# Adding a bias by accumulating DMAs at the end of a decoder trunk, and sharing one normalisation between two engines

## The chip, the cores and the metric

The kernel runs on one core of a Trainium2 chip. The core has five engines with instruction streams of their own: TensorE (PE; its weight loads are listed apart as PEld), VectorE (DVE), ScalarE (ACT), GpSimd (POOL) and SyncE (SP, which here only issues DMAs). Sixteen DMA engines move data between HBM and the on-chip memory (SBUF). Matmuls write their results to a third memory, PSUM. The metric is the device time of one execution in microseconds; the kernel before takes 1242.96 us (median of three runs, 1242.6 to 1243.46).

## The reference

A two-layer trunk for 256 tokens of width 2048. Layer 0 is a Mamba-2 mixer, layer 1 a dilated windowed attention; between them the residual stream gives one shared K and V. Each layer ends in the same layer norm. Cut to what the change touches:

```
def _layer_norm(x, g, b):
    mu = jnp.mean(xf, -1, keepdims=True)
    var = jnp.mean(jnp.square(xf - mu), -1, keepdims=True)
    return ((xf - mu) * lax.rsqrt(var + LN_EPS)) * g + b
...
for layer in range(DEPTH):
    shift, scale, gate = _adaln(c, ada_w[layer], ada_b[layer])
    h = x * (1.0 + scale) + shift
    y = _ssd_mixer(h, ...) if layer == 0 else _dilated_mixer(h, k_sh, v_sh, ...)
    x = _layer_norm(ALPHA * x + (1.0 + gate) * y, ln_g[layer], ln_b[layer])
    if layer == 0:
        k_sh, v_sh = _shared_kv(x, kv_w)
```

The output is the second layer norm: for each token the normalised row, times `ln_g[1]`, plus `ln_b[1]`.

## The kernel before

All matrix products are made from float32 operands split into a rounded high part and a remainder. `split` (L95 to L102) does this for each weight piece of 128x1024: ACT writes `whi` (L99), DVE writes `wlo` (L101). The helpers `tm_mults` (L212 to L214) and `cm_wide` (L181, L184) multiply the pieces. Weight pieces come in one after the other on SP's DMA queue.

The 256 tokens are handled as two blocks b = 0 and b = 1 of 128 rows; block b holds the tokens 2j + b, so that a block's rows are every second row of the output. `u[0]` and `u[1]` hold the residual stream of the two blocks, 128x2048 each; in the instruction listings they are `u_5515` and `u_5516`. A chunk is 512 of the 2048 columns.

The order of the instructions on each engine is fixed when the program is built. It follows the code, except that a scheduler may move an instruction ahead of others that it doesn't depend on; `tc.issue_after(x)` tells it to keep what is built inside behind the instruction x. At run time each engine works through its list in order and waits on semaphores.

Two places matter here.

The first is the end of layer 0. `residual` (L798 to L800) makes gate times product plus residual for each chunk and collects its statistics; `moments` (L802 to L813) turns these into a factor and an offset per row. `normalise(b, c0_, c1_)` (L819 to L824) applies them to some columns: on ACT (L822) or on DVE (L824). The first 512 columns of a block are normalised in two calls of 256 columns, the other 1536 columns later in three calls. Then `x_quad(b)` has TensorE transpose the first four 128-column tiles (L885), ACT write their scaled high part (L887), ACT or DVE write the full value (L890, L892), and DVE the remainder (L893). With that, the products for V begin: `high` (L915) and `low` (L920) multiply the four tiles by weight pieces split in advance, first for block 0, then for block 1. After that a loop over q = 2 to 7 goes on with `split` and `tm_mults`, and `x_tile` makes the further tiles, two for each q (L871, L874 to L876).

The second is the end of the kernel. The last products of block 0 end earlier than those of block 1. `r0, nb0` are block 0's factor and offset: ACT normalises its four chunks (L1138), and for each chunk DVE multiplies by `ln_g[1]` (`scaled`, L1105), DVE adds `ln_b[1]` (L1158), and SP stores the chunk (L1130). At the same time block 1 is finished: its last products, its residual (L798, L799), its statistics (L800), and `moments`. Three of block 1's chunks take another way: TensorE adds up the scaled residual and minus the mean (L1151, L1155) in PSUM, and one DVE instruction applies the factor and adds `ln_b[1]` (`whole`, L1163). The fourth is normalised by ACT (L1160), multiplied by DVE (L1105) and added to by DVE (L1170). `lnt[:, 0]` and `lnt[:, 1]` hold `ln_g[1]` and `ln_b[1]`, repeated on all 128 partitions (L1119); in the listings they are part of `actT`.

Of the kernel before, what the change touches and what calls it, by code (L numbers as in the profile page):

```python
# [13 lines left out]
ALU = mybir.AluOpType  # L14
# [35 lines left out]
def trunk(ctx, tc, xT, x, c, par, cst, bias, lnrow, ada, wdt, win, wxs, wout, wk, wv, wbin, wbout, out):  # L50
    nc = tc.nc
    V, S, T, PO = nc.vector, nc.scalar, nc.tensor, nc.gpsimd
# [9 lines left out]
    def bcast(dst, src, off=0):  # L62
        nc.sync.dma_start(dst, bass.AP(tensor=src.tensor, offset=src.offset + off,
                                       ap=[[0, P], [1, dst.shape[-1]]]))
# [22 lines left out]
    def rows(t, b):  # L87

        return t.rearrange("(j r) n -> r j n", r=2)[b]

    def load_piece(src):
        raw = wp.tile([P, 1024], F32, name="raw", bufs=6)
        nc.sync.dma_start(raw, src)
        return raw

    def split(raw, into=None, after=None):

        hi, lo = into or [wp.tile([P, 1024], F32R, name=n, bufs=4) for n in ("whi", "wlo")]
        copied.append(S.activation(hi, raw, AF.Copy))  # L99
        with tc.issue_after(after) if after is not None else ExitStack():  # L100
            latest.append(V.tensor_tensor(lo, raw, hi.bitcast(F32), op=ALU.subtract))  # L101
        return hi.rearrange("p (k n) -> p k n", k=2), lo.rearrange("p (k n) -> p k n", k=2)  # L102
# [114 lines left out]
    def tm_pair():  # L217
        return [mm.tile([P, 512], F32, name="acc") for _ in range(2)]
# [92 lines left out]
    def queue(pool, cols):  # L311

        loaded = [ada_load(pool, *cols[0])]

        def step(i):
            raw = loaded.pop(0)
            if i + 1 < len(cols):
                loaded.append(ada_load(pool, *cols[i + 1]))
            ada_dot(*cols[i], raw)

        jobs.extend(lambda i=i: step(i) for i in range(len(cols)))

    def drain():
        while jobs:
            jobs.pop(0)()
# [8 lines left out]
    with ExitStack() as cA:  # L334
# [458 lines left out]
        u = [pu.tile([P, D], F32, name=f"u{b}") for b in range(2)]  # L793
# [24 lines left out]

        def normalise(b, c0_, c1_):  # L819
            (r, nb), cs_ = norm[b], slice(c0_, c1_)  # L820
            if b == 0 or c1_ <= 512:
                S.activation(u[b][:, cs_], u[b][:, cs_], AF.Identity, bias=nb, scale=r)  # L822
            else:
                V.tensor_scalar(u[b][:, cs_], u[b][:, cs_], r, nb, op0=ALU.mult, op1=ALU.add)  # L824
# [76 lines left out]
    def evict_v(hq, g, ps):  # L901
        vt[hq, g] = place(3 * hq + g if hq == 0 else 9 + g, [P, 2, 512])
        with behind_next():
            for b in range(2):
                S.activation(vt[hq, g][:, b, :], ps[b], AF.Copy)

    with ExitStack() as cL:
        pl = cL.enter_context(tc.tile_pool(name="pl", bufs=3))

        vps = [tm_pair(), tm_pair()]  # L910
        def high(i, b):
            for k in range(2):
                kt = 2 * (i // 2) + k
                for w in first_v[i]:
                    T.matmul(vps[i % 2][b], hx(kt)[:, b * P:b * P + P], w[:, k, :], start=kt == 0 and w is first_v[i][0],  # L915
                             stop=False)

        def low(i, b):
            for k in range(2):
                T.matmul(vps[i % 2][b], lx(2 * (i // 2) + k)[:, b * P:b * P + P], first_v[i][0][:, k, :], start=False,  # L920
                         stop=False)

        end, _ = x_quad(0)
        with tc.issue_after(end.ins):
            for n in range(1, 4):
                normalise(0, 512 * n, 512 * n + 512)
        for i in range(4):
            high(i, 0)
        for i in range(4):
            if i == 2:  # L930
                _, tile4 = x_quad(1)
                for n in range(1, 4):
                    normalise(1, 512 * n, 512 * n + 512)
            low(i, 0)
        for i in range(4):
            high(i, 1)
            if i == 2:
                x_tile(4)
                x_tile(5)
        for i in range(4):  # L940
            low(i, 1)
        for q in range(2, KT // 2):
            if q < KT // 2 - 1:
                x_tile(2 * q + 2)
                x_tile(2 * q + 3)
            for j in range(2):
                w = split(load_piece(wv[2 * j][q]), after=tile4.ins if q == 2 else None)
                tm_mults(q, w, vps[j], hx, lx, 0, KT, range(2))
        for g in range(2):
            evict_v(0, g, vps[g])  # L950

        R = (1, 2)
        pin[0] = latest[-1].ins
        with tc.issue_after(tile4.ins):
            state[0] = 0
            queue(pl, cols1[11:])
            jobs.append(lambda: gate_out(1))
            upcoming.extend((wk[2 * (2 * g + hq) + w], 0) for hq in range(2) for g in range(NG) for w in range(2))
            upcoming.extend((wv[1 + 2 * g], 0) for g in range(NG))
            evict_v(0, 2, tm_chunk(wv[4], hx, lx, rate=R))  # L960
            for hq in range(2):
                for g in range(NG):
                    kv[hq, g] = place(3 + 3 * hq + g, [P, 4, L])
                    for w in range(2):
                        cm_wide(wk[2 * (2 * g + hq) + w], kv[hq, g][:, 2 * w:2 * w + 2, :], rate=R, later=True)
            for g in range(NG):
                evict_v(1, g, tm_chunk(wv[1 + 2 * g], hx, lx, rate=R))
            drain()
            late = latest[-1].ins

        ada_bias(1, slice(0, KT), slice(0, 2))
        for kt in range(KT):
            t = pl.tile([P, L], F32, name="htmp")
            S.activation(t, xhi[:, kt, :].bitcast(F32), AF.Identity, bias=shift(1, kt), scale=scale(1, kt))
            V.scalar_tensor_tensor(t, xlo[:, kt, :].bitcast(F32), scale(1, kt), t, op0=ALU.mult, op1=ALU.add)
            split_act(xhi[:, kt, :], xlo[:, kt, :], t)
# [119 lines left out]
    gt, lnt = gl[:, 0], gl[:, 1]  # L1096
# [19 lines left out]
    for i in range(2):  # L1116
        hold(6 + i)
        with tc.issue_after(latest[-1].ins):
            bcast(lnt[:, i, :], lnrow, (2 + i) * D)  # L1119
    for n in range(2):  # L1120
        scaled(1, chunk[n])
    ps = [tm_pair() for _ in range(2)]
# [6 lines left out]
    def store(b, c):  # L1129
        nc.sync.dma_start(rows(out, b)[:, c], u[b][:, c])  # L1130
# [12 lines left out]
    for h in range(2):  # L1143
        end = last(1, 1, slice(256 * h, 256 * h + 256), halves[h])
# [10 lines left out]
        T.matmul(pt, diag, lnt[:, 0, c], start=False, stop=True)  # L1155
    for c in chunk:
        scaled(0, c)
        V.tensor_tensor(u[0][:, c], u[0][:, c], lnt[:, 1, c], op=ALU.add)  # L1158
        store(0, c)
    S.activation(u[1][:, chunk[3]], u[1][:, chunk[3]], AF.Identity, bias=nb1, scale=r1)  # L1160

    def whole(n):
# [100 lines left out]
```

## Time and profile before

| | |
|---|---|
| median of 3 runs | 1242.96 us (1242.6 to 1243.46) |
| the profiled execution | 1243.02 us, of which its span takes 1241.2 us |
| TensorE busy | 1216.1 us, 98% of the span |
| VectorE busy | 1028.3 us, 83% |
| ScalarE busy | 702.4 us, 57% |
| GpSimd busy | 0.2 us, 4 instructions |
| granted TensorE clock | 1.0 over the whole execution |

A row of the timeline reads: start in us from the span's start, duration in us, engine, line of the kernel, operation, what is written from what, number of instructions merged into the row, and in brackets how long the engine stood idle before it and what ended the wait. On one engine successive instructions overlap a little, so that they start closer together than their durations say. A row with SPq is the issue of a DMA, not its transfer; the time "to landing" is given apart. In the row of a window the columns are its length, the busy time and number of instructions of PE, PEld, DVE, ACT and POOL, then the granted clock, the mean busy share of the DMA engines, and the GB/s that they moved.

### The profile page before, as it was taken

To read this page: it belongs to the slowest core of one execution; us is meant where nothing else is said; L and a number is where in the kernel's file an instruction comes from. 1 tells how busy PE (TensorE), PEld (TensorE's weight loads), DVE (VectorE), ACT (ScalarE), POOL (GpSimd) and SP (SyncE) were. 2 spreads that over 40 slices of the span, in tenths; PEclk is the share of its full clock that TensorE was granted. 3 is DMA by queue.
4 is the path that set the end of the run, shared out by engine and by line. 5 is a ranking of instruction groups with operands and counts; after the bars stand their busy time and mean duration, and the time that the engine had idled before them with its cause. 6 is when DMAs were issued, how large, how long until landed. Compare 5 with 4: busy or idle time off the path is not lost.

```text
span 1241.2 us, 18711 instructions
## 1 busy us (share of the span) xinstructions
PE 1216.1 (98%) x7078; PEld 1043.9 (84%) x7078; DVE 1028.3 (83%) x1454; ACT 702.4 (57%) x1045; POOL 0.2 (0%) x4
## 2 busy tenths in 40 slices
PE   4999999999999999999999999999999999999997
PEld 4989988898888888888888788888888888888886
DVE  5999986999988989899768678889978867658777
ACT  3555477868597789764345544434435644444631
POOL 0000000000000000000000000000000000000000
PEclk9999999999999999999999999999999999999999
DMA  9999977687656456699998569989997774463751
GB/s 384 421 423 422 421 270 245 226 295 257 213 193 208 166 172 202 214 338 346 356 320 293 192 199 381 353 340 368 380 375 294 229 263 132 136 205 118 233 175 68
DMA packets 80587, 335.88 MB, mean 271 GB/s; under 512 B 9105, under 2 KB 9329, under 8 KB 67697
## 3 DMA queue, kind: packets, MB, share of 16 engines
q1 hardware_dynamic: 80496, 334.69, 74.9%
q8 instruction: 55, 0.90, 0.3%
q14 instruction: 36, 0.29, 0.1%
HBM read 332.47 MB, written 2.18 MB: 270 GB/s over the span
## 4 chain that ended last, share of the span: by engine, by line
PE 83%; DMA 8%; DVE 6%; ACT 2%; issue 1%; DVEq 0%; ACTq 0%; SPq 0%
PE acc L181 24%; PE acc L184 12%; PE acc L213 12%; PE acc L214 12%; PE acc L212 11%; DMA raw<-in_win 6%; DVE wlo L101 2%; PE acc L150 2%; PE acc L152 2%; PE acc L151 2%; PE py L705 1%; DVE araw L295 1%; DMA araw<-in_ada 1%; ACT whi L99 1%; PE acc L915 1%
## 5 line engine op out<-in xcount | busy, mean ns | idle before, releaser
L99 ACT ACTIVATE whi<-raw 128x1024 fp32r<-128x1024 f32 x390 | 409.5, 1058 | 355.5 <-PE acc L214 137.5
L101 DVE TENSOR_TENSOR wlo<-raw,whi 128x1024 fp32r<-128x1024 f32 x390 | 470.3, 1221 | 142.9 <-ACT whi L99 138.4
L181 PE MATMUL acc<-actT,whi 128*128 128x512 f32 x1280 | 405.3, 397 | 0.0
L184 PEld LDWEIGHTS acc<-actT,wlo 128*128 128x128 f32 x1280 | 239.4, 188 | 55.6 <-DVE wlo L101 0.4
L213 PE MATMUL acc<-wlo,actT 128*128 128x512 f32 x656 | 257.1, 392 | 0.8 <-DVE wlo L101 0.8
L212 PE MATMUL acc<-whi,actT 128*128 128x512 f32 x656 | 253.3, 394 | 0.0
L184 PE MATMUL acc<-actT,wlo 128*128 128x256 f32 x1280 | 252.9, 279 | 0.0
L295 DVE SCALAR_TENSOR_TENSOR araw<-araw,cb__72 128x2048 f32<-128x2048 f32 x96 | 219.3, 2285 | 9.9 <-DMA araw<-in_ada 9.8
L181 PEld LDWEIGHTS acc<-actT,whi 128*128 128x128 f32 x1280 | 195.9, 189 | 0.4
L214 PE MATMUL acc<-whi,actT 128*128 128x512 f32 x432 | 169.0, 391 | 0.0
L213 PEld LDWEIGHTS acc<-wlo,actT 128*128 128x128 f32 x656 | 123.2, 188 | 27.2 <-DVE wlo L101 2.1
L212 PEld LDWEIGHTS acc<-whi,actT 128*128 128x128 f32 x656 | 122.7, 188 | 24.1
L150 PE MATMUL acc<-actT,whi 128*128 128x256 f32 x376 | 106.9, 286 | 0.0
L151 PE MATMUL acc<-actT,whi 128*128 128x256 f32 x376 | 106.1, 284 | 0.0
L152 PE MATMUL acc<-actT,wlo 128*128 128x256 f32 x376 | 104.6, 285 | 0.4 <-DVE wlo L101 0.4
L214 PEld LDWEIGHTS acc<-whi,actT 128*128 128x128 f32 x432 | 81.1, 188 | 16.7
L214 PE MATMUL acc<-whi,ylo 128*128 128x512 f32 x224 | 87.5, 391 | 0.0
L150 PEld LDWEIGHTS acc<-actT,whi 128*128 128x128 f32 x376 | 72.7, 193 | 0.6
L151 PEld LDWEIGHTS acc<-actT,whi 128*128 128x128 f32 x376 | 72.7, 193 | 0.4
L152 PEld LDWEIGHTS acc<-actT,wlo 128*128 128x128 f32 x376 | 71.5, 193 | 0.7 <-DVE wlo L101 0.6
L214 PEld LDWEIGHTS acc<-whi,ylo 128*128 128x128 f32 x224 | 42.1, 188 | 8.6
L663 ACT ACTIVATE seg<-cbc,cumT 128x128 f32<-128x128 f32 x128 | 41.0, 389 | 5.1 <-DVE wlo L101 2.3
(278 smaller groups left out, 1124.2 us busy)
## 6 DMA issues: line engine op xcount, KB each, us to landing
araw<-in_ada SPq DMA_DIRECT2D x96, 1024.0 KB, 7.4
raw<-in_win SPq DMA_DIRECT2D x112, 512.0 KB, 6.7
raw<-in_wout SPq DMA_DIRECT2D x64, 512.0 KB, 5.9
raw<-in_wbin SPq DMA_DIRECT2D x64, 512.0 KB, 4.2
raw<-in_wxs SPq DMA_DIRECT2D x48, 512.0 KB, 4.6
raw<-in_wv SPq DMA_DIRECT2D x48, 512.0 KB, 6.7
raw<-in_wk SPq DMA_DIRECT2D x48, 512.0 KB, 7.6
cbc<-cumd SPq DMA_DIRECT2D x16, 512.0 KB, 5.0
```

The lines of the kernel that those rows point to most:

```text
L99: copied.append(S.activation(hi, raw, AF.Copy))
L101: latest.append(V.tensor_tensor(lo, raw, hi.bitcast(F32), op=ALU.subtract))
L150: T.matmul(o, hi[:, k, c_], ahi[:, kt, :], start=first, stop=False, skip_group_check=True)
L151: T.matmul(o, hi[:, k, c_], alo[:, kt, :], start=False, stop=False, skip_group_check=True)
L152: T.matmul(o, lo[:, k, c_], ahi[:, kt, :], start=False, stop=kt == k1 - 1, skip_group_check=True)
L181: T.matmul(ps[n], hi[:, k, n * P:n * P + P], both(kt), start=kt == 0, stop=False, skip_group_check=True)
L184: T.matmul(ps[n][:, 0, :], lo[:, k, n * P:n * P + P], high(kt), start=False, stop=kt == KT - 1, skip_group_check=True)
L212: T.matmul(o, h_, hi[:, k, :], start=kt == k0, stop=False, skip_group_check=part)
L213: T.matmul(o, h_, lo[:, k, :], start=False, stop=False, skip_group_check=part)
L214: end = T.matmul(o, l_, hi[:, k, :], start=False, stop=kt == k1 - 1, skip_group_check=part)
L295: return V.scalar_tensor_tensor(raw, raw, 1.0, cb_, op0=ALU.mult, op1=ALU.mult, accum_out=mod[layer][:, ct, j:j + 1])
L663: S.activation(seg[:, hh, b, :], cbc[:, hh, b, :], AF.Relu, bias=cumT[:, b, h0 + hh:h0 + hh + 1], scale=-1.0)
```

## The change

Three edits.

1. In `normalise`, for block 0, the second 256 columns are now normalised by DVE and not by ACT. The first 256 stay on ACT.
2. In the loop over q, everything that `split` builds is held behind `end`, the last of the four L890 instructions of `x_quad(0)`.
3. At the end, block 0's half of the output in HBM is filled with `ln_b[1]` by one DMA on SP's queue, issued behind the load of `lnt[:, 1]` and waiting for it (1 MB). For each chunk of block 0, DVE still multiplies by `ln_g[1]`, but no longer adds; GpSimd issues a DMA of 128x512 elements that adds the products to what stands in the output. The four stores of block 0 on SP are gone.

```
@@ normalise
-            if b == 0 or c1_ <= 512:
+            if c1_ <= 256 if b == 0 and c0_ < 512 else b == 0 or c1_ <= 512:
                 S.activation(u[b][:, cs_], u[b][:, cs_], AF.Identity, bias=nb, scale=r)
             else:
                 V.tensor_scalar(u[b][:, cs_], u[b][:, cs_], r, nb, op0=ALU.mult, op1=ALU.add)
@@ the loop over q
             for j in range(2):
-                w = split(load_piece(wv[2 * j][q]), after=tile4.ins if q == 2 else None)
+                with tc.issue_after(end.ins):
+                    w = split(load_piece(wv[2 * j][q]), after=tile4.ins if q == 2 else None)
                 tm_mults(q, w, vps[j], hx, lx, 0, KT, range(2))
@@ the end
             bcast(lnt[:, i, :], lnrow, (2 + i) * D)
+    nc.sync.dma_start(rows(out, 0), lnt[:, 1, :])
...
     for c in chunk:
         scaled(0, c)
-        V.tensor_tensor(u[0][:, c], u[0][:, c], lnt[:, 1, c], op=ALU.add)
-        store(0, c)
+        nc.gpsimd.dma_start(rows(out, 0)[:, c], u[0][:, c], accum_op=ALU.add)
```

After the second edit the lines behind L947 have a number higher by one, after the third edit by two; `scaled` is L1106 in the changed kernel.

ScalarE at the end of layer 0, before: `e0nb, e0y` and `e1nb, e1y` are the offsets and factors of block 0 and block 1; a row with x2 stands for two instructions.

```order
L99 ACTIVATE whi<-raw 128x1024 x7
L822 ACTIVATE u_5515<-u_5515,e0nb,e0y 128x256 x2
L99 ACTIVATE whi<-raw 128x1024
L887 ACTIVATE actT<-aux,prm 128x128 x4
L890 ACTIVATE xq<-aux,prm 128x128 x4
L822 ACTIVATE u_5515<-u_5515,e0nb,e0y 128x512 x2
L822 ACTIVATE u_5516<-u_5516,e1nb,e1y 128x256 x2
L822 ACTIVATE u_5515<-u_5515,e0nb,e0y 128x512
L887 ACTIVATE actT<-aux,prm 128x128 x4
L99 ACTIVATE whi<-raw 128x1024
L874 ACTIVATE actT<-aux,prm 128x256 x4
```

The same place on ScalarE in the changed kernel:

```order
L99 ACTIVATE whi<-raw 128x1024 x5
L822 ACTIVATE u_5515<-u_5515,e0nb,e0y 128x256
L887 ACTIVATE actT<-aux,prm 128x128 x4
L890 ACTIVATE xq<-aux,prm 128x128 x4
L822 ACTIVATE u_5515<-u_5515,e0nb,e0y 128x512 x2
L822 ACTIVATE u_5516<-u_5516,e1nb,e1y 128x256 x2
L822 ACTIVATE u_5515<-u_5515,e0nb,e0y 128x512
L887 ACTIVATE actT<-aux,prm 128x128 x4
L99 ACTIVATE whi<-raw 128x1024 x3
L874 ACTIVATE actT<-aux,prm 128x256 x2
L99 ACTIVATE whi<-raw 128x1024
```

Three L99 have moved from ahead of the first L887 to behind the second group of L887; one L822 is gone to VectorE, where it stands right behind block 0's offset (L812).

VectorE at the end of the kernel, before (`e1mv` is block 1's mean and variance, `po` and `acc` are products in PSUM):

```order
L1158 TENSOR_TENSOR u_5515<-u_5515,actT 128x512
L800 BN_STATS st_5518<-u_5516 128x6
L1105 TENSOR_TENSOR u_5515<-u_5515,actT 128x512
L798 TENSOR_TENSOR actT<-po,actT 128x256
L1158 TENSOR_TENSOR u_5515<-u_5515,actT 128x512
L799 SCALAR_TENSOR_TENSOR u_5516<-u_5516,actT 128x256
L1105 TENSOR_TENSOR u_5515<-u_5515,actT 128x512
L800 BN_STATS st_5518<-u_5516 128x6
L1158 TENSOR_TENSOR u_5515<-u_5515,actT 128x512
L805 BN_AGGR e1mv<-st_5518 128x2
```

The same place on VectorE in the changed kernel:

```order
L798 TENSOR_TENSOR actT<-acc,actT 128x256
L1106 TENSOR_TENSOR u_5516<-u_5516,actT 128x512
L799 SCALAR_TENSOR_TENSOR u_5516<-u_5516,actT 128x256
L1106 TENSOR_TENSOR u_5515<-u_5515,actT 128x512
L800 BN_STATS st_5518<-u_5516 128x6
L798 TENSOR_TENSOR actT<-po,actT 128x256
L799 SCALAR_TENSOR_TENSOR u_5516<-u_5516,actT 128x256
L800 BN_STATS st_5518<-u_5516 128x6
L805 BN_AGGR e1mv<-st_5518 128x2
```

The four L1158 are gone, and the last multiplication of block 0 now stands ahead of block 1's last residual part (`L798 actT<-po`). Behind `moments` the order is also another one: before, two L1163, then L1105 and the third L1163; in the changed kernel one L1163, then L1106 (which waits for ACT's normalisation of block 1's fourth chunk), then the other two L1164. On SP the four stores of `u_5515` give way to one DMA of 128x2048 from `actT`, issued behind the last load of `ln_b[1]`; on POOL there are four DMAs `out<-u_5515 128x512`, the first of which waits for that fill.

More of the change, by code (lines that the diff above doesn't have):

```diff
@@ L820, in normalise @@
             (r, nb), cs_ = norm[b], slice(c0_, c1_)
[L821 removed]
+            if c1_ <= 256 if b == 0 and c0_ < 512 else b == 0 or c1_ <= 512:
                 S.activation(u[b][:, cs_], u[b][:, cs_], AF.Identity, bias=nb, scale=r)
@@ L946, in trunk @@
             for j in range(2):
-                w = split(load_piece(wv[2 * j][q]), after=tile4.ins if q == 2 else None)
+                with tc.issue_after(end.ins):
+                    w = split(load_piece(wv[2 * j][q]), after=tile4.ins if q == 2 else None)
                 tm_mults(q, w, vps[j], hx, lx, 0, KT, range(2))
@@ L1157, in trunk @@
         scaled(0, c)
-        V.tensor_tensor(u[0][:, c], u[0][:, c], lnt[:, 1, c], op=ALU.add)
-        store(0, c)
+        nc.gpsimd.dma_start(rows(out, 0)[:, c], u[0][:, c], accum_op=ALU.add)
     S.activation(u[1][:, chunk[3]], u[1][:, chunk[3]], AF.Identity, bias=nb1, scale=r1)
```

1 line of the change is left out of this document (added).

## The prediction

> **What bounds the kernel now.** I read the page's first part, then the windows, then the timeline of the two places that the change touches, engine by engine.
>
> ```profile
> PE 1216.1 (98%) x7078; PEld 1043.9 (84%) x7078; DVE 1028.3 (83%) x1454; ACT 702.4 (57%) x1045; POOL 0.2 (0%) x4
> ...
> sum 480.00, PE 479.57 PEld 412.11 DVE 375.13 ACT 228.23 POOL 0.00; mean PE 39.96 PEld 34.34 DVE 31.26 ACT 19.02 POOL 0.00
> ```
>
> The first line is the page's: TensorE is busy for 98% of the span. The second is the sum of twelve windows of 40 us from 735 to 1215 us: TensorE is idle there for 0.43 us in all. So between the change's two places nothing but TensorE's own work sets the pace, and time can only be won or lost where TensorE waits: at the end of layer 0, and behind its last product. The end of layer 0, ACT, DVE and PE (a row's columns: start, duration, engine, line, what is written from what):
>
> ```profile
> 698.59 1.09 ACT L822 ACTIVATE u<-u,e0nb,e0y 128x256 f32<-128x256 f32 x2 [0.62 <-DVE e0nb L812]
> 699.59 1.04 ACT L99 ACTIVATE whi<-raw 128x1024 fp32r<-128x1024 f32 x1
> 700.53 1.48 ACT L887 ACTIVATE actT<-aux,prm 128x128 fp32r<-128x128 f32 x4
> ...
> 704.68 1.10 ACT L822 ACTIVATE u<-u,e1nb,e1y 128x256 f32<-128x256 f32 x2
> 705.68 0.81 ACT L822 ACTIVATE u<-u,e0nb,e0y 128x512 f32<-128x512 f32 x1
> 706.60 1.51 ACT L887 ACTIVATE actT<-aux,prm 128x128 fp32r<-128x128 f32 x4
> 704.49 0.16 DVE L812 SCALAR_TENSOR_TENSOR e1nb<-e1mv,e1y 128x1 f32<-128x1 f32 x1
> 699.43 0.74 PE L885 MATMUL aux<-cc,u 128*128 128x128 f32 x4
> 701.02 3.95 PE L915 MATMUL acc<-s,actT 128*128 128x512 f32 x16 [0.85 <-ACT actT L887]
> 707.11 3.04 PE L915 MATMUL acc<-s,actT 128*128 128x512 f32 x12
> ```
>
> The bracket in the L915 row is TensorE's one long wait between the layers: 0.85 us for ACT's first tile (L887), which stands behind a weight split (L99). The end of the kernel, DVE:
>
> ```profile
> 1223.40 0.69 DVE L1105 TENSOR_TENSOR u<-u,actT 128x512 f32<-128x512 f32 x1 [0.89 <-ACT u L1138]
> ...
> 1224.62 0.68 DVE L1158 TENSOR_TENSOR u<-u,actT 128x512 f32<-128x512 f32 x1
> 1225.21 0.69 DVE L799 SCALAR_TENSOR_TENSOR u<-u,actT 128x512 f32<-128x512 f32 x1
> ...
> 1228.28 0.69 DVE L1158 TENSOR_TENSOR u<-u,actT 128x512 f32<-128x512 f32 x1
> 1228.88 0.42 DVE L800 BATCH_NORM_STATS2 st<-u 128x6 f32<-128x256 f32 x1
> 1229.22 0.68 DVE L1105 TENSOR_TENSOR u<-u,actT 128x512 f32<-128x512 f32 x1
> 1229.81 0.42 DVE L798 TENSOR_TENSOR actT<-po,actT 128x256 f32<-128x256 f32 x1
> 1230.14 0.68 DVE L1158 TENSOR_TENSOR u<-u,actT 128x512 f32<-128x512 f32 x1
> 1230.74 0.42 DVE L799 SCALAR_TENSOR_TENSOR u<-u,actT 128x256 f32<-128x256 f32 x1
> 1231.08 0.69 DVE L1105 TENSOR_TENSOR u<-u,actT 128x512 f32<-128x512 f32 x1
> 1231.68 0.42 DVE L800 BATCH_NORM_STATS2 st<-u 128x6 f32<-128x256 f32 x1
> 1232.02 0.68 DVE L1158 TENSOR_TENSOR u<-u,actT 128x512 f32<-128x512 f32 x1
> 1232.61 0.29 DVE L805 BATCH_NORM_AGGREGATE e1mv<-st 128x2 f32<-128x30 f32 x1
> 1232.93 0.29 DVE L807 TENSOR_SCALAR sc<-cc,e1mv 128x128 f32<-128x128 f32 x1
> ...
> 1234.85 0.16 DVE L812 SCALAR_TENSOR_TENSOR e1nb<-e1mv,e1y 128x1 f32<-128x1 f32 x1
> 1234.92 1.40 DVE L1163 SCALAR_TENSOR_TENSOR u<-aux,e1y,actT 128x512 f32<-128x512 f32 x2
> 1236.24 0.68 DVE L1105 TENSOR_TENSOR u<-u,actT 128x512 f32<-128x512 f32 x1
> 1236.84 0.74 DVE L1163 SCALAR_TENSOR_TENSOR u<-po,e1y,actT 128x512 f32<-128x512 f32 x1
> 1237.50 0.68 DVE L1170 TENSOR_TENSOR u<-u,actT 128x512 f32<-128x512 f32 x1
> ```
>
> From 1223.40 no row has a wait: DVE works without a gap to 1237.50 + 0.68 = 1238.18, a 512-column instruction every 0.60 us and a 256-column one every 0.34 us. Behind it come only the last store and the program's end. So DVE's work is the path here, as long as its inputs are there. PE and ACT, which give them:
>
> ```profile
> 1229.03 0.28 PE L214 MATMUL po<-whi,s 128*128 128x256 f32 x1
> ...
> 1230.86 1.02 PE L1151 MATMUL po<-u,cc 128*128 128x512 f32 x2
> 1233.27 1.98 PE L1155 MATMUL aux<-actT,sc 128*128 128x512 f32 x4 [1.39 <-DVE e1ve L809]
> ...
> 1235.04 0.81 ACT L1160 ACTIVATE u<-u,e1nb,e1y 128x512 f32<-128x512 f32 x1 [9.55 <-DVE e1nb L812]
> ```
>
> And the DMAs: the last load of SP's queue and how long such loads take to land, a window behind it (the last two columns are the DMA engines' busy share and GB/s), the stores, and the slowest load of a store's size (KB each, then us to landing):
>
> ```profile
> 1187.84 1.31 SPq L63 DMA_DIRECT2D actT<-in_lnrow  x1
> ...
> DMA to landing us min/median/max: 7.3/8.8/10.9
> ...
> 1205.00:1210.00 5.00, 5.00 (x23) 4.13 (x23) 3.30 (x5) 0.00 (x0) 0.00 (x0) 1.00 0.01 3
> ...
> out<-u SPq DMA_DIRECT2D x8, 256.0 KB, 2.0
> xt<-in_xT SPq DMA_DIRECT2D x8, 256.0 KB, 11.8
> ```
>
> **The change, part by part.** The sum is made against the profiled execution: 1243.02 us, of which 1241.2 are span; the median of the runs is 0.06 us below it.
>
> *End of layer 0.* ACT's path to the first tile is now one L822 (698.59 to about 699.18) and then L887. The L99 that ran at 699.59 and two earlier ones are behind the second L887 group. DVE's new 256-column L824 takes about 0.35 us (half of a 512-column instruction) at 698.6, where DVE waited for block 1's products anyway. PE's four transposes, which start at 699.43 because PE was still multiplying, were done at 699.43 + 0.74 = 700.17; the last two had waited for ACT's second L822. L887 can start at about 700.1 and not 700.53: at most 0.45 us for L915. This doesn't last: block 1's offset (L812, 704.49) hangs on block 1's products, which have not moved. From it ACT has two L822 of 256 and one of 512 ahead of the second L887 group, 704.65 + 1.0 + 0.8 = 706.4 against 706.60. So 0.2 us remain for the second L915. The three late L99 take ACT from about 707.8 to 710.7, ahead of the L874 that was at 710.41 before: 0.3 us later, which I cost at nothing, because PE is inside the L915 and L920 of block 1 until 713.5; without that cover it would cost its 0.3 us. **Term 1: -0.2 us**, between -0.45 (all of the first gain) and +0.1. It has to survive 500 us, and with 0.43 us of idle TensorE in 480 it should.
>
> *The fill.* The last load was issued by 1187.84 + 1.31 and landed at the latest 10.9 us after 1187.84, at 1198.7. No row shows a 1 MB write; by the loads of the same size (7.3 to 10.9 us) it is over by 1209.6 at the latest, and the DMA engines are idle there (share 0.01). Its queue, SP, has nothing behind it but the stores of block 1, more than 20 us later. DVE's first product is there at 1224.1, 14 us after it. Cost nothing; the cover is those 14 us, and TensorE at 100% meanwhile.
>
> *DVE without the adds.* Four L1158 of 0.60 us are gone, 2.4 us. Two of them stood ahead of the `L798 actT<-po` at 1229.81, but the L1105 of 1231.08 now stands ahead of it as well: 1229.81 - 2 x 0.60 + 0.60 = 1229.21. PE's last product ends at 1229.03 + 0.28 = 1229.31, so DVE waits for it for the first time, to about 1229.34. Then L798, L799, L800 in a row, each needing the one before: 0.42 + 0.03 each, so L805 starts at 1230.70, against 1232.61: 1.91 us earlier. L805 to L812 and to the first L1163 keep their distances (2.24 and 2.31 us): 1232.94 and 1233.01. What is late next: PE must have finished L1151 (1230.86 + 1.02 = 1231.88; the next one can be issued 0.16 us earlier) before L1155, which now starts at about 1231.72 and not 1233.27, and gives the first pair about 1.0 us later, 1232.75, in time for 1233.01. ACT is not in time: L1160 starts behind L812's end, 1233.13, and takes 0.81 to 1233.94, and its reader L1105 is now second and not third behind `moments`. It would stand at 1233.01 + 0.70 = 1233.71 and starts at 1233.97, a new wait of 0.26 us. Then 0.60 for it, 0.66 each for the last two L1163, and L1170 at 1235.89, against 1237.50. **Term 2: -1.6 us**, between -1.9 (without the new wait) and -1.2 (both new waits twice as long).
>
> *The accumulating DMAs.* POOL has done nothing so far and has nothing else to do; its first DMA waits for the fill and the product at 1224.1, the others for theirs. The products of the four chunks come at about 1224.1, 1225.3, 1226.5 and 1229.0 (L1105 now at 1228.29 + 0.68). No row shows a DMA issued by POOL, nor one that adds. From below it is a store of the same size, 2.0 us; from above the slowest load of that size, 11.8 us. I take 4 us, near the store, because the DMA engines are idle but for it, and twice the store, because it must also read what it adds to. The fourth then lands at 1233.0. The last store of block 1 is issued at 1235.89 + 0.68 = 1236.57 and lands 2.0 later, 1238.6. So the additions are covered by 5.6 us; at 11.8 us the fourth would land at 1240.8 and not 1238.6, +2.2. **Term 3: 0**, between 0 and +2.2. The Trainium skill has a price for it, in *DMA: Bandwidth & Descriptors*, section "Anatomy of one DMA — SWDGE (gpsimd) path": about 2.0 us and bytes at 436 GB/s, an estimate of 2.6 us for 256 KB, by which the sum would be the same; no run here shows it yet.
>
> Sum: -0.2 - 1.6 + 0 = -1.8 us, 1243.02 - 1.8 = 1241.2 us, also against the median. That is 0.15%. A difference of 0.2%, 2.5 us, is about what a measurement of this kernel can tell from no change, so my forecast is "within 0.2%", on the fast side.
>
> **The rivals.**
>
> *POOL can't get its DMAs out beside DVE.* This is the case on the other side. DVE's run without a gap goes to 1236.57; if POOL's writing of its DMAs were held up until then, the four would go out one after the other, 2.0 us each, and the last land at 1244.6. The program's end then comes 1.0 us later (a span of 1241.2 less the 1238.18 + 2.0 of the last store now), a span of 1245.6: +4.4, less term 1: 1247.2 us. The same comes out if an addition takes some 5 us and they don't overlap: 1224.1 + 20 = 1244.1. It decides from the fourth landing at 1238.6; from 1240.2 the kernel is slower than before, from 1242.7 by over 0.2%. For it speaks that POOL shows no DMA in this trace; against it that the first chunk has 14 us. The Trainium skill, in *SBUF — State Buffer*, section "Who interferes with whom", says that a DMA issued by GpSimd is held up where VectorE runs in a mode with two ports, and that an instruction with two SBUF inputs disturbs only GpSimd's reads; by that rule the L1105, L799 and L1163 here would not hold it up. Chance 0.20.
>
> *The additions eat a part.* They land between 1238.7 and 1242.7, at 10 us each or half overlapped: 1241.4 to 1245.4 us, 1243 in the middle. Chance 0.12.
>
> *More than the sum.* ACT is in time for L1105 (-1.9), the first 0.45 us last, and the 0.43 us of idle TensorE in between go too: -2.8, 1240.2 us. Against it: two of the three need an input earlier than its producer's row gives it. Chance 0.07.
>
> **How the numbers follow.** The forecast has 0.61 and lies between 1240.7 (-1.9 - 0.45) and 1242.0 (-1.2 + 0.1). The range takes it, the third rival and the middle of the second, 1240.1 to 1244.5: 0.61 + 0.07 + about 0.10, near 8 in 10; the first rival is what is left out. Slower by over 0.2% (above 1245.4): the first rival, most of it, 0.19. Faster by over 0.2% (below 1240.5): 0.06. Within: 0.75.
>
> **What would show it.** Right: no bracket above 0.1 us before the L915 row at 701; L805 of block 1 about 1.9 us closer to PE's last product, with a wait for PE ahead of `L798 actT<-po` and one for ACT ahead of the last L1106; four POOL issues between 1224 and 1231, landing by 1235; SP's end waiting for the store of `u[1]`. Wrong: an end that waits for `out<-u` of POOL's queue, DVE instructions at the end longer than 0.69 us beside POOL, or a fill that lands after 1224.

## The result

| | median | range | runs |
|---|---|---|---|
| before | 1243.06 us | 1242.6 to 1244.53 | 20 |
| changed | 1241.22 us | 1240.06 to 1241.85 | 20 |

The changed kernel takes 0.9984 of the time before, with a 95% interval of 0.9978 to 0.999: 1.84 us less. That is inside the bound of 0.2% that the prediction named, on the fast side. The profiled execution took 1240.81 us, 1239.0 of them span (before: 1243.02 and 1241.2).

### The profile page after: what moved, and what is told of

Same layout as the page of the kernel before. It is cut to its first block, busy times and chain, and to the rows that moved or that the text cites. A ratio compares the mean times of both kernels' runs of the same rounds, so it can differ in the third digit from the quotient of the medians.

```text
span 1239.0 us, 18712 instructions
## 1 busy us (share of the span) xinstructions
PE 1214.5 (98%) x7078; PEld 1041.6 (84%) x7078; DVE 1027.9 (83%) x1451; ACT 701.5 (57%) x1044; POOL 3.8 (0%) x8
## 4 chain that ended last, share of the span: by engine, by line
PE 86%; DVE 5%; DMA 4%; ACT 2%; issue 1%; SPq 0%; DVEq 0%; ACTq 0%
PE acc L181 24%; PE acc L213 12%; PE acc L214 12%; PE acc L184 12%; PE acc L212 12%; DMA araw<-in_ada 2%; PE acc L150 2%; PE acc L152 2%; PE acc L151 2%; DVE araw L295 2%; DVE wlo L101 2%; PE py L705 1%; DMA raw<-in_win 1%; ACT whi L99 1%; PE acc L915 1%
## 5 line engine op out<-in xcount | busy, mean ns | idle before, releaser
L99 ACT ACTIVATE whi<-raw 128x1024 fp32r<-128x1024 f32 x390 | 409.6, 1058 | 360.5 <-PE acc L214 131.6
L212 PE MATMUL acc<-whi,actT 128*128 128x512 f32 x656 | 253.4, 394 | 0.0
L214 PE MATMUL acc<-whi,actT 128*128 128x512 f32 x432 | 168.9, 391 | 0.0
L212 PEld LDWEIGHTS acc<-whi,actT 128*128 128x128 f32 x656 | 122.7, 188 | 24.2
L214 PEld LDWEIGHTS acc<-whi,actT 128*128 128x128 f32 x432 | 81.1, 188 | 16.5
L214 PE MATMUL acc<-whi,ylo 128*128 128x512 f32 x224 | 87.5, 391 | 0.0
L214 PEld LDWEIGHTS acc<-whi,ylo 128*128 128x128 f32 x224 | 42.1, 188 | 8.6
```

The costliest lines, as they stand in the source:

```text
L212: T.matmul(o, h_, hi[:, k, :], start=kt == k0, stop=False, skip_group_check=part)
L214: end = T.matmul(o, l_, hi[:, k, :], start=False, stop=kt == k1 - 1, skip_group_check=part)
```

## The profile after

The busy line of the changed kernel's page, and the sum of the same twelve windows from 735 to 1215 us:

```profile
PE 1214.5 (98%) x7078; PEld 1041.6 (84%) x7078; DVE 1027.9 (83%) x1451; ACT 701.5 (57%) x1044; POOL 3.8 (0%) x8
...
sum 480.00, PE 479.67 PEld 412.24 DVE 375.53 ACT 228.16 POOL 0.00; mean PE 39.97 PEld 34.35 DVE 31.29 ACT 19.01 POOL 0.00
```

TensorE is idle for 0.33 us in those 480 us, as good as before (0.43). What happened is again at the two places. Two profiles start with a scatter of some tenths of a microsecond, so positions are compared as distances: at the first place from the start of TensorE's last L214 ahead of the transposes, at the second from the start of its last L214 of all.

The end of layer 0 in the timeline of the changed kernel, first block 0, then block 1:

```profile
699.01 0.40 PE L214 MATMUL acc<-whi,ylo 128*128 128x512 f32 x1
699.24 0.60 PE L885 MATMUL aux<-cc,u 128*128 128x128 f32 x4
699.88 1.50 ACT L887 ACTIVATE actT<-aux,prm 128x128 fp32r<-128x128 f32 x4 [0.88 <-PE aux L885]
700.39 3.93 PE L915 MATMUL acc<-s,actT 128*128 128x512 f32 x16 [0.55 <-ACT actT L887]
703.08 0.68 DVE L893 TENSOR_TENSOR actT<-xq,actT 128x512 fp32r<-128x512 f32 x1
704.12 0.16 DVE L812 SCALAR_TENSOR_TENSOR e1nb<-e1mv,e1y 128x1 f32<-128x1 f32 x1
704.32 1.09 ACT L822 ACTIVATE u<-u,e1nb,e1y 128x256 f32<-128x256 f32 x2
705.32 0.80 ACT L822 ACTIVATE u<-u,e0nb,e0y 128x512 f32<-128x512 f32 x1
705.52 0.38 PE L885 MATMUL aux<-cc,u 128*128 128x128 f32 x2
706.02 1.48 ACT L887 ACTIVATE actT<-aux,prm 128x128 fp32r<-128x128 f32 x4
706.52 3.04 PE L915 MATMUL acc<-s,actT 128*128 128x512 f32 x12
712.93 0.47 PE L212 MATMUL acc<-whi,actT 128*128 128x512 f32 x1
```

Those rows of the kernel before that the prediction has not shown:

```profile
699.20 0.39 PE L214 MATMUL acc<-whi,ylo 128*128 128x512 f32 x1
703.44 0.69 DVE L893 TENSOR_TENSOR actT<-xq,actT 128x512 fp32r<-128x512 f32 x1
706.18 0.38 PE L885 MATMUL aux<-cc,u 128*128 128x128 f32 x2
713.53 0.47 PE L212 MATMUL acc<-whi,actT 128*128 128x512 f32 x1
```

L887 now waits for the transposes and no longer for ScalarE's L99. The first L915 starts 1.38 us behind the L214 (before 1.82, so 0.44 sooner), the second 7.51 (7.91, 0.40 sooner), and the first L212 of the next stage 13.92 (14.33, 0.41 sooner). TensorE still waits for the first tile, 0.55 us: the L887 behind the transposes takes its time, whoever made way for it. The second L915 shows no bracket, but the load of its weights (PEld), which stands ahead of it, also waits for L887. The waits of these loads, first before, then in the changed kernel (us in total, times, longest); the longest belongs to the first L915, and 0.3 us remain for the second:

```profile
PEld acc L915 <- ACT actT L887: 1.4, 2, 1.1
...
PEld acc L915 <- ACT actT L887: 1.1, 2, 0.8
```

The end of the changed kernel: TensorE's last product, VectorE behind it, the products and ScalarE that feed it, and GpSimd's DMA issues:

```profile
1228.27 0.28 PE L214 MATMUL po<-whi,s 128*128 128x256 f32 x1
1228.59 0.42 DVE L798 TENSOR_TENSOR actT<-po,actT 128x256 f32<-128x256 f32 x1
1229.05 0.43 DVE L799 SCALAR_TENSOR_TENSOR u<-u,actT 128x256 f32<-128x256 f32 x1
1229.51 0.43 DVE L800 BATCH_NORM_STATS2 st<-u 128x6 f32<-128x256 f32 x1
1229.97 0.29 DVE L805 BATCH_NORM_AGGREGATE e1mv<-st 128x2 f32<-128x30 f32 x1
1230.97 1.88 PE L1157 MATMUL aux<-actT,sc 128*128 128x512 f32 x4
1232.42 0.81 ACT L1161 ACTIVATE u<-u,e1nb,e1y 128x512 f32<-128x512 f32 x1 [7.68 <-DVE e1nb L812]
1233.26 0.69 DVE L1106 TENSOR_TENSOR u<-u,actT 128x512 f32<-128x512 f32 x1 [0.20 <-ACT u L1161]
1235.19 0.68 DVE L1171 TENSOR_TENSOR u<-u,actT 128x512 f32<-128x512 f32 x1
...
1223.93 1.89 POOL L1160 DMA_DIRECT2D out<-u  x2 [1223.49 <-DVE actT L798]
1226.04 0.86 POOL L1160 DMA_DIRECT2D out<-u  x1 [0.22 <-issue]
1228.51 0.86 POOL L1160 DMA_DIRECT2D out<-u  x1 [1.61 <-DVE u L1106]
```

VectorE's last add (L1171) starts 6.92 us behind TensorE's last L214, before 8.47: 1.55 us sooner. From there to the end of the span it is 3.85 us, before 3.73 (by the spans that the traces hold, 1239.043 and 1241.234 us). So the sum is -0.41 at the end of layer 0, -1.55 behind TensorE's last product and +0.12 behind the last add: -1.84 us, the difference of the medians. That the two agree to a hundredth is chance, since the interval of the ratio is some 0.7 us to either side. The spans differ by 0.35 us more (2.19), which is scatter between the two places (515.34 us from that L212 to the last L214, before 515.50) and at the start (0.19).

The DMA issues of the last 50 us (KB each, median us to landing), the shortest, middle and longest landing of L1160, and what SP waits for at the program's end (us in total, times, longest):

```profile
out<-actT SPq DMA_DIRECT2D x1, 1024.0 KB, 3.8
out<-u POOLq DMA_DIRECT2D x4, 256.0 KB, 5.3
out<-u SPq DMA_DIRECT2D x4, 256.0 KB, 2.1
...
DMA to landing us min/median/max: 4.2/5.3/5.9
...
SPq L1260 <- DMA out<-u: 1.6, 3, 0.7
```

The fill took 3.8 us, 20 us ahead of its first reader. The fourth accumulating DMA, issued at 1228.51, had landed at about 1233.2 (4.7 us), block 1's last store at about 1238.0: the additions are covered by nearly 5 us.

## The experiments

Ten kernels ran. Eight of them have 11 timed runs each, in two groups of four, each group on a chip of its own and beside 33 runs of the kernel before (median 1243.35 and 1243.2 us). The last two have one run each, and only the distances in their traces are used. The ratios have intervals of some 1 us to either side, and they and the quotients of the medians differ by up to 0.0006, so of small differences the distances in the traces decide, which repeat to some hundredths of a microsecond. All of them (us; the first three columns of times are taken from the last L214 of layer 0, the next two from the last L214 of all, the end from the span that the trace holds to a nanosecond):

| kernel | first L915 | second L915 | L212 | last add | end of span | median, to before |
|---|---|---|---|---|---|---|
| before | 1.82 | 7.91 | 14.33 | 8.47 | 12.20 | |
| changed | 1.38 | 7.51 | 13.92 | 6.92 | 10.77 | -1.84 |
| changed, again | 1.38 | 7.50 | 13.90 | 6.92 | 10.75 | -1.96 |
| the tail alone | 1.83 | 7.86 | 14.29 | 6.91 | 10.76 | -1.60 |
| the middle alone | 1.38 | 7.51 | 13.91 | 8.48 | 12.19 | -0.97 |
| additions left out | 1.38 | 7.51 | 13.91 | 6.92 | 10.66 | -1.72 |
| adds kept, GpSimd stores | 1.38 | 7.51 | 13.92 | 8.47 | 12.37 | -0.56 |
| one accumulating DMA | 1.38 | 7.50 | 13.93 | 6.91 | 12.05 | -0.69 |
| last chunk accumulated too | 1.39 | 7.52 | 13.94 | none | 12.04 | -0.56 |
| other order | 1.38 | 7.50 | 13.91 | 6.63 | 10.43 | -1.78 |
| sharing alone | 2.28 | 8.32 | 14.61 | 8.48 | 12.18 | -0.65, one run |
| hold alone | 1.52 | 7.58 | 13.99 | 8.46 | 12.19 | -0.68, one run |

### The two places apart

Edits 1 and 2 undone, against the changed kernel:

```
-            if c1_ <= 256 if b == 0 and c0_ < 512 else b == 0 or c1_ <= 512:
+            if b == 0 or c1_ <= 512:
...
-                with tc.issue_after(end.ins):
-                    w = split(...)
+                w = split(...)
```

> The fill and the accumulating DMAs without the two edits at the end of layer 0. My theory: the four additions that leave VectorE carry the gain; L805 starts 1.9 us sooner after the last 1.50 us L798 product than before (2.64 less 0.76 in the two profiles), the last L1171 1.5 us sooner, and the time is 1.5 us below before, 0.3 us above the changed kernel. Rival, the middle carries it: no difference from before. Rival, the two parts hang together (a POOL issue that is only covered because the layer's end is earlier): less than 1 us below before.

And edit 3 undone (no fill, the adds of `ln_b[1]` on VectorE, block 0's stores on SP):

```
-    nc.sync.dma_start(rows(out, 0), lnt[:, 1, :])
...
-        nc.gpsimd.dma_start(rows(out, 0)[:, c], u[0][:, c], accum_op=ALU.add)
+        V.tensor_tensor(u[0][:, c], u[0][:, c], lnt[:, 1, c], op=ALU.add)
+        store(0, c)
```

> The two edits at the end of layer 0 without the fill and the accumulating DMAs. The prediction kept 0.2 us of them; by the traces of before and after it is 0.4 us (second L915 0.59 us earlier, 0.19 of it by the start). My theory: 0.4 us below before, with the second L915 and the first L212 of the next stage each 0.4 us sooner after the last L214 ahead of the transposes, and the last store as before. Rival, the prediction's own step: 0.2 us. Rival, the 0.4 us of the traces are scatter: no change in those distances.

The tail alone: 1241.75 us against 1243.35, a ratio of 0.9987 (0.9979 to 0.9996). Its last add stands at 6.91 us and its end at 10.76, as in the changed kernel; its layer 0 ends as before. The middle alone: 1242.38 us, ratio 0.9998 (0.9989 to 1.0007), which tells nothing by itself; but its L212 stands at 13.91 us, 0.42 sooner than before, and its tail as before. So the two parts add up, 1.4 us of span behind the last product and 0.4 us at the end of layer 0, and neither needs the other. The 0.2 us that the prediction kept of the middle are too few.

### Does the gain come from the adds, and do the additions cost anything?

Fill and accumulation left out; block 0's products go out by SP's stores. Block 0's bias is missing from this output.

```
-    nc.sync.dma_start(rows(out, 0), lnt[:, 1, :])
...
-        nc.gpsimd.dma_start(rows(out, 0)[:, c], u[0][:, c], accum_op=ALU.add)
+        store(0, c)
```

> The changed kernel without the fill and without the accumulation: block 0's products go out by plain stores of SP, and the bias of block 0 is left out of the output, so this part of the computation is missing. VectorE has the same instructions as in the changed kernel. My theory (additions and fill cost nothing): within 0.2 us of the changed kernel, L805, L1171 and the end of VectorE at the same distances from PE's last product. Rival, the additions eat a part: faster than the changed kernel by that part, up to 1 us. Rival, SP's queue has now four stores more and the stores of block 1 get out later: slower by some tenths.

And the adds back on VectorE, no fill, plain GpSimd stores:

```
-        nc.gpsimd.dma_start(rows(out, 0)[:, c], u[0][:, c], accum_op=ALU.add)
+        V.tensor_tensor(u[0][:, c], u[0][:, c], lnt[:, 1, c], op=ALU.add)
+        nc.gpsimd.dma_start(rows(out, 0)[:, c], u[0][:, c])
```

> The changed kernel with the four additions back on VectorE, no fill, and block 0's sums stored by plain GpSimd DMAs instead of SP's. My theory: what counts is VectorE's four instructions of 0.69 us, not the queue; L805 and L1171 stand as before after PE's last products, and the time is 0.4 us below before, by the middle alone (1.5 above the changed kernel). Its GpSimd stores price the same path without accumulation: if the accumulation makes the landing of 4.2 to 5.9 us in the changed kernel long, they land in 2 to 3 us; if it is the GpSimd path, in 4 to 6. Rival, the gain comes from SP's queue being relieved of four stores: 1 us or more below before although the additions are back.

Without any addition the last add stands where it does in the changed kernel (6.92 us), and the end is 0.09 to 0.11 us nearer (10.66 against 10.77 and 10.75); 1241.63 us, ratio 0.9985 (0.9977 to 0.9994). So fill and additions together cost at most about 0.1 us. With the adds back on VectorE the whole gain of the tail is gone (8.47 us), though SP's queue has no store of block 0: 1242.79 us, ratio 0.9998 (0.9989 to 1.0006). The gain is that of VectorE's four instructions, not of the queue. One GpSimd issue of this kernel, the row of its four GpSimd DMAs, and their landings (L1160):

```profile
1226.19 0.67 POOL L1160 DMA_DIRECT2D out<-u  x1 [1225.74 <-DVE u L799]
...
out<-u POOLq DMA_DIRECT2D x4, 256.0 KB, 2.3
...
DMA to landing us min/median/max: 2.3/2.3/2.4
```

A plain GpSimd store of 256 KB takes 0.54 to 0.67 us to issue and 2.3 to 2.4 to land, 0.2 to 0.4 more than SP's; with the addition it is 0.86 to 1.0 and 4.2 to 5.9. What makes it long is the addition, not the engine that issues it. The end of the span was 12.37 us here, 0.16 to 0.19 later than in the kernels with the adds on VectorE and SP's stores. So the 0.1 us behind the last add in the changed kernel need no addition either: from the last add to the end it is 3.71 to 3.75 us in the five kernels here whose GpSimd issues no DMA, and 3.81 to 3.90 in this one and in the four with four accumulating DMAs. Why stays open.

### What the additions cost when nothing covers them

One accumulating DMA behind all four products:

```
     for c in chunk:
         scaled(0, c)
-        nc.gpsimd.dma_start(rows(out, 0)[:, c], u[0][:, c], accum_op=ALU.add)
+    nc.gpsimd.dma_start(rows(out, 0), u[0], accum_op=ALU.add)
```

> The changed kernel with one accumulating DMA of 128x2048 (1 MB) behind all four products in place of four of 256 KB. VectorE's and ScalarE's instructions stay as they are; the one DMA can be issued from 1228.2 to 1228.5 on, as the fourth was. The four landed 4.2 to 5.9 us after their issue, while 108 to 172 GB/s were moved. Theory, the accumulation has a price by the byte and was hidden: at some 109 GB/s the 1 MB takes 9.6 us, behind an issue of 0.9 us or more it lands at 1239 to 1240, later than the last store of block 1 (1238.0), and the kernel ends 1 to 2 us later than the changed one, with SP's end waiting for GpSimd's write. Rival, the accumulation has a fixed price by the DMA: it lands 5 to 6 us after 1228.5 (plus 1.8 us for the bytes, by the 3.8 us against 2.0 us of the plain writes), by 1236, and the time is the changed kernel's.

1242.51 us, 1.27 above the changed kernel beside it (1241.24); in the trace the end is 1.28 us later (12.05 against 10.77) with the last add in its place (6.91). From its views of DMA issues, of windows (last two columns: busy share of the DMA engines, GB/s), of the queues that moved anything from 1234.6 to 1235.3 us (packets, MB, share of the DMA engines), and of waits at SP's end:

```profile
1228.73 1.00 POOL L1160 DMA_DIRECT2D out<-u  x1 [1228.28 <-PE po L214]
...
out<-u POOLq DMA_DIRECT2D x1, 1024.0 KB, 8.0
out<-u SPq DMA_DIRECT2D x4, 256.0 KB, 3.5
...
1233.00:1235.00 2.00, 0.64 (x2) 0.00 (x0) 1.81 (x3) 0.16 (x1) 0.00 (x0) 1.00 1.06 221
...
q0 software_dynamic: 18, 0.15, 101.1%
...
SPq L1260 <- DMA out<-u: 2.7, 4, 1.0
```

The time came as the theory had it, but not in its way. The 1 MB landed 8.0 us after its issue, at about 1236.7, earlier than the 1239 to 1240 expected and ahead of block 1's last store (about 1239.3). What was late were block 1's own stores: 3.4 to 4.4 us to land in place of 2.0 to 2.1. The DMA engines were full (1.06), and with the addition alone: the one queue that moves anything from 1234.6 to 1235.3 is GpSimd's (q0), though SP had issued block 1's first two stores at 1233.02 and 1234.57. The rival was near with the landing (by 1236) and wrong with the time. So an accumulating DMA that isn't yet over delays the stores beside it, before it is itself the last. In the changed kernel the additions begin early, and the fourth has landed (about 1233.2) before block 1's first store, issued at 1233.09, moves anything (from 1233.9 on).

Block 1's fourth chunk filled and accumulated as well:

```
     nc.sync.dma_start(rows(out, 0), lnt[:, 1, :])
+    nc.sync.dma_start(rows(out, 1)[:, 1536:2048], lnt[:, 1, 1536:2048])
...
-    V.tensor_tensor(u[1][:, chunk[3]], u[1][:, chunk[3]], lnt[:, 1, chunk[3]], op=ALU.add)
-    store(1, chunk[3])
+    nc.gpsimd.dma_start(rows(out, 1)[:, chunk[3]], u[1][:, chunk[3]], accum_op=ALU.add)
```

> The changed kernel with block 1's fourth chunk of the output also filled with the bias ahead of time and its product added by a fifth accumulating DMA, so that the last add of VectorE (0.68 us) goes too. Its product is there at 1233.95 (L1106), GpSimd starts 0.3 to 0.6 us later, and 4.2 to 5.9 us after that it has landed: 1238.4 to 1240.5, while the other last store is 0.66 us earlier than in the changed kernel (1237.4). Theory: the accumulating DMA that nothing hides sets the end; 0.4 to 2.5 us slower than the changed kernel, and VectorE's add is the cheaper one there. Rival, the end goes by VectorE alone as long as any landing is under 6 us: 0.4 to 0.7 us faster than the changed kernel.

1242.64 us, 1.40 above the changed kernel beside it, and 1.28 later in the trace, though VectorE ends a whole instruction sooner. The fifth accumulating DMA and its landing, the landings of block 1's three plain stores (L1133), and SP's wait at the end:

```profile
1233.88 0.86 POOL L1172 DMA_DIRECT2D out<-u  x1 [4.88 <-DVE u L1106]
...
DMA to landing us min/median/max: 4.5/4.5/4.5
...
DMA to landing us min/median/max: 2.0/2.3/4.0
...
SPq L1260 <- DMA out<-u: 3.5, 2, 3.0
```

The theory has the time right, and the way only in part. The addition takes 4.5 us with no other addition beside it and lands at about 1238.4, and SP waits 3.5 us for the output and not 1.6. But what lands last is a plain store again: block 1's last one, issued at 1234.93 beside the addition, takes 4.0 us in place of 2.1 and lands at about 1238.9. Without this delay the addition would have been the last, about 0.6 us sooner and still some 0.7 us later than the changed kernel's last store, an estimate from these landings. The rival is out: the addition is under 6 us, and the kernel is slower all the same. The same exchange of an add for an accumulating DMA that gains 1.55 us for block 0 loses 1.28 for the last chunk, because there nothing is left to do behind it.

### VectorE's new wait for ScalarE

`scaled(1, chunk[3])` held behind the second `whole`:

```
     whole(0)
-    whole(1)
-    scaled(1, chunk[3])
+    with tc.issue_after(whole(1).ins):
+        scaled(1, chunk[3])
     whole(2)
```

(`whole` returns its instruction for this.)

> The changed kernel with the product of block 1's last chunk held behind the second fused one, so that VectorE does not wait 0.20 us for ScalarE. Theory: the wait is on the path that sets the end; the last add starts 0.2 us sooner after PE's last product (6.72 in place of 6.92 us) and the time is 0.2 us below the changed kernel's, less than the timing tells apart. Rival: the wait moves to the first or third fused product, which waits for TensorE's L1157 instead; no change.

> The changed kernel itself, beside the three others on the same chip. 1.8 us below before (1.2 to 2.4); accumulating DMAs land 4 to 6 us after issue again.

```profile
1232.95 1.41 DVE L1164 SCALAR_TENSOR_TENSOR u<-aux,e1y,actT 128x512 f32<-128x512 f32 x2
1234.27 0.68 DVE L1106 TENSOR_TENSOR u<-u,actT 128x512 f32<-128x512 f32 x1
...
1235.54 0.68 DVE L1172 TENSOR_TENSOR u<-u,actT 128x512 f32<-128x512 f32 x1
```

The two L1164 now stand ahead of the L1106, which has no wait any more, and the last add is at 6.63 us, 0.29 sooner than in the changed kernel; the end at 10.43, 0.32 to 0.34 sooner. That is more than the wait of 0.20: two L1164 in a row take 1.41 us, and 0.75 each with the L1106 between them. So the wait was on the path. The times can't show it: 1241.42 us, ratio 0.9988 (0.9979 to 0.9996), against 1241.24 us, 0.9984 (0.9975 to 0.9992), of the changed kernel beside it, whose additions landed after 4.5 to 6.0 us. By the trace this is the best of the kernels here, by the timing it is as good as the changed one.

### Which edit frees the first tile

Edit 1 alone (sharing), then edit 2 alone (hold), on the kernel before:

```
-            if b == 0 or c1_ <= 512:
+            if c1_ <= 256 if b == 0 and c0_ < 512 else b == 0 or c1_ <= 512:
```

> Of the two edits at the end of layer 0 only the shared normalisation (columns 256 to 512 of block 0 on VectorE); the late L99 of ScalarE stays where it is. Read by distances from TensorE's last L214 ahead of the transposes, since one look can't tell 0.4 us in the time. Before: first L887 1.33 us behind that L214, first L915 1.82, second L915 7.91, first L212 14.33; changed: 0.87, 1.38, 7.51, 13.92. Theory, the hold is what frees ScalarE for L887: the transposes are done earlier but L887 waits for the L99 of 1.04 us that stands ahead of it, and the distances are those of before within 0.1 us. Rival, the sharing does it: the changed kernel's distances. A third way: L99 now starts earlier, in the place of the second L822, and part of the 0.4 us comes without the hold.

```
-                w = split(...)
+                with tc.issue_after(end.ins):
+                    w = split(...)
```

> Of the two edits at the end of layer 0 only the weight pieces held behind the end of the normalisation; both normalisations stay on ScalarE (1.09 us, to 0.5 us behind the start of the last L214). Theory: the four transposes end 0.97 us behind that L214 as before, L887 can follow at once, so most of the 0.4 us is there with the hold alone: first L887 about 1.0 us behind it (before 1.33, changed 0.87), second L915 7.6 to 7.7. Rival, both are needed: the distances of before.

ScalarE and TensorE with the sharing alone, whose L214 starts at 698.76:

```profile
698.66 1.99 ACT L99 ACTIVATE whi<-raw 128x1024 fp32r<-128x1024 f32 x2
...
700.55 1.49 ACT L887 ACTIVATE actT<-aux,prm 128x128 fp32r<-128x128 f32 x4
701.04 3.92 PE L915 MATMUL acc<-s,actT 128*128 128x512 f32 x16 [1.45 <-ACT actT L887]
```

And with the hold alone, whose L214 starts at 699.31:

```profile
700.32 1.50 ACT L887 ACTIVATE actT<-aux,prm 128x128 fp32r<-128x128 f32 x4 [0.53 <-PE aux L885]
700.83 3.93 PE L915 MATMUL acc<-s,actT 128*128 128x512 f32 x16 [0.55 <-ACT actT L887]
```

The times, 1242.77 us with the sharing and 1242.74 with the hold against 1243.42 before, one run each, can't tell them apart. The hold alone gives 0.34 of the 0.41 us, as expected. The sharing alone missed all three expectations: it makes the first L915 0.46 us later than before and L212 0.28 later. In the room that the moved L822 leaves on ScalarE the scheduler puts an L99 of 1 us that stood behind the second group of L887 before, and the first L887 stands behind two of them. It gains its 0.1 us only together with the hold.

The shift of the first L915 reaches the second nearly whole in each of them: -0.44 and -0.40 with both edits, -0.30 and -0.33 with the hold, +0.46 and +0.41 with the sharing. But it is not one path in all three. With the hold alone the second L887 follows block 1's transposes as before (706.38, 0.42 us behind the L885 at 705.96; before 706.60 and 706.18). With both edits it follows ScalarE's L822 (706.02, 0.50 behind that L885). With the sharing alone the second L915 stands 0.68 us behind its L887 (707.08 and 706.40) and not 0.5, because the scheduler has put block 1's four transposes together and more of block 0's products behind them.

## Why the prediction came out as it did

The forecast was 1241.2 us, the median is 1241.22. Its terms were -0.2, -1.6 and 0, measured -0.41, -1.55 and +0.12; errors of opposite sign cancel (0.2 us too little for the end of layer 0, nearly as much too much for the end of the kernel), and that the sum hits the median to 0.02 us is luck. The mechanism of the large term was right.

- **End of layer 0, first tile.** "at most 0.45 us for L915": 0.44. But the sign given for it, "no bracket above 0.1 us before the L915 row", was wrong: 0.55 us stay. By the prediction's own numbers L887 could start at 700.1 at the earliest, and in its rows the first L915 stands half a microsecond behind L887 (701.02 and 700.53), so 700.6 was the earliest for it, some 0.4 us behind the transposes; the sign contradicted the step.
- **End of layer 0, second tile.** This is the mis-sized term: 0.2 us were kept, 0.41 came. The step that failed is "This doesn't last: block 1's offset (L812, 704.49) hangs on block 1's products, which have not moved". The second L915 starts half a microsecond behind its L887 in both kernels, so L887 counts. Before, it followed block 1's transposes (706.60 behind 706.18 + 0.38). These stand in TensorE's own list behind block 0's products and moved with the first L915; they would have let L887 start at about 705.94 in the changed kernel. It starts at 706.02, right behind ScalarE's L822 (705.32 + 0.80). So ScalarE's list does bound the second tile there, as the prediction had it, and its 0.2 us to spare were read rightly. But the offset at the head of that list moved as well: L812 stands 5.29 us behind the last L214 before and 5.11 in the changed kernel, because L893 ahead of it in VectorE's list no longer waits for ScalarE's L890 (which ended at 703.41 before, just ahead of L893 at 703.44, and at 702.78 in the changed kernel, 0.30 ahead of it). 0.2 us to spare and 0.18 from the offset make the 0.40. That 0.2 us would have been all with an unmoved offset is worked out from these rows; no run holds the offset back.
- **Three late L99.** Cost nothing, as said: L212 is as much earlier as the second L915.
- **VectorE without the adds.** L805 stands 1.70 us behind TensorE's last product, before 3.58: 1.88 for the 1.91 worked out, with L798 `actT<-po` right behind TensorE's last product (1228.59, and 1228.27 + 0.28), as the prediction had it. The new wait for ScalarE is 0.20 us for 0.26, and the other order shows that it is paid in full and more. L1171 is 1.55 us sooner for 1.61.
- **The accumulating DMAs.** Right that they are hidden, and 4 us was short: 4.2 to 5.9. The cover is nearly 5 us, not the 5.6 named. Left out of the sum were the 0.1 us behind the last add, and the way in which the cover would fail: not by a landing that comes last, from 1238.6 on, but earlier, by block 1's stores, which the DMA engines serve late while an addition goes on. The Trainium skill's fit (*DMA: Bandwidth & Descriptors*, section "Anatomy of one DMA — SWDGE (gpsimd) path"), an estimate of 2.6 us, is near the plain GpSimd stores' 2.3 to 2.4 and well below the accumulating ones.
- **The fill.** 3.8 us and over 20 us before it was needed: nothing, as said.
- **The rival on the other side.** GpSimd gets its DMAs out beside VectorE: the first is issued 0.6 us after its product's end at 1223.34, and VectorE's instructions stay at 0.68 to 0.69 us. The rule of the Trainium skill (*SBUF — State Buffer*, section "Who interferes with whom"), by which these instructions would not hold up GpSimd's DMAs, agrees.
- **More than the sum.** One of its three parts came (the gain of the first tile lasts), the other two not: ScalarE was not in time, and the time between the two places did not change beyond its scatter (515.34 us for 515.50; 515.20 to 515.55 over all the kernels here).

## What to carry to other kernels

When an engine is the path behind the last product, work that it does for data which is ready early can go to a DMA that adds in HBM, as long as the DMA is over before the last stores begin; for the data that is ready last the same exchange loses. A shift at one wait of the bounding engine is passed on to all that stands behind it in that engine's own list, so look there first, and then at what the lists of the engines that feed it have to spare: here ScalarE's had 0.2 us, and the rest of the gain came through because what it waited for came sooner too. Work taken off a queue that a scheduler fills leaves room that other work takes: hold that other work, and try the two edits apart.

## What was not expected of the hardware

An accumulating DMA costs about twice a plain one: 256 KB took 4.5 us with no other addition beside it, against 2.0 to 2.1 for plain stores of SP and 2.3 to 2.4 of GpSimd, and 1 MB took 8.0 us against 3.8 for the fill. From these two pairs (both accumulating ones had stores of block 1 beside them, and the rows of the 1 MB are 8 KB long, those of the 256 KB 2 KB) an estimate is 3.3 us plus the bytes at some 225 GB/s with the addition (3.5 us for 768 KB more), and 1.5 us plus the bytes at about 450 GB/s without (1.7 to 1.8 us more). While it runs, plain stores beside it take up to 4.4 us in place of 2.0 to 2.1: 3.4 to 4.4 beside the 1 MB, 2.3 and 4.0 beside the 256 KB. GpSimd's issue of one is 0.86 to 1.0 us, of a plain store 0.54 to 0.67.
